# A two-layer decoder trunk on one core: layer 0 with three pairs by token halves, twelve early products and three-pass downs; layer 1 with pairs 0 and 1 by seven, low results by VectorE

## The chip, the core and the metric

The kernel runs on one core of one Trainium2 chip. A core has TensorE (PE) for matmuls, with its weight loads (PEld) shown apart; VectorE (DVE), ScalarE (ACT) and GpSimd (POOL) for elementwise work; and SyncE (SP), which here only issues DMAs. Each engine works through its own queue in order; semaphores make it wait for others. The metric is the device time of one execution in microseconds (us), lower is better.

## What is computed

512 tokens (S) of 1024 channels (D) in float32 go through two layers. Cut to what matters:

```python
h = h + conformer_conv(rmsnorm(h, g0), ...)     # layer 0: pw1, GLU, 31-tap causal conv, LayerNorm, silu, pw2
h = h + swiglu_ffn(rmsnorm(h, g1), w_up[0], w_down[0])
k, v = split(rmsnorm(h, g_kv) @ w_kv)
q = rmsnorm(h, g2) @ w_q                        # layer 1: windowed attention with sinks and a bias
h = h + banded_sink_attention(q, k, v, sinks, rel_bias) @ w_o
h = h + swiglu_ffn(rmsnorm(h, g3), w_up[1], w_down[1])
return rmsnorm(h, g_final)

def swiglu_ffn(x, w_up, w_down):
    gate, up = split(x @ w_up, 2)
    return (silu(gate) * up) @ w_down           # hidden width 2816
```

The change touches the two feed-forward networks (FFN) and what runs beside them.

## The kernel before

**Pairs and chunks.** The 2816 hidden columns are worked on as 11 pairs of 256 columns. Weights come as chunks of 128 x 1024 floats (512 KB) in a list written out beforehand, `PLAN` (`chunk_plan`): 258 chunks. `load` (L261) issues each as a DMA on SP's queue into one of six `raw` buffers, up to nine chunks ahead of use. ScalarE then rounds a chunk to its high half `whi` (L294), and VectorE subtracts to get the low half `wlo` (L297), three chunks ahead of use. A product is made of three passes of TensorE, high by high, high by low and low by high (`mm3`, L380, L381, L382). `get` and `get_seven` hand out the next chunk and call `advance`, which issues loads, splits and a share of the weight sums.

**By seven.** A pair's up matmul can be done directly, four chunks of 24 matmuls on 512 tokens, or "by seven": the weight blocks A11, A12, A21, A22 and the activation blocks B are combined as in Strassen's method into seven products, each of one chunk (24 matmuls of 256 tokens). The combinations are named in

```python
SEVEN = ("A11 B11", "S1 T1", "S2 T2", "A12 B21", "S3 T3", "S4 B22", "A22 T4")
```

S1 to S4 are sums of weight blocks. They are made in DRAM ahead of time by `prepare`: a copy on SP's queue (L275) and a DMA on POOL's queue that adds the other block (L289). `share[0]` says how many such sums are started per chunk used. Some copies are made early in larger pieces (`EARLY`). T1 to T4 are sums of activation blocks. The products of a pair are added up in PSUM chains and in an `up` tile (`SevenPair.take`), then gated (`gates`).

**Layer 0.** After pw1 and the convolution, the tokens are done in two halves of 256. `HALVES0` names which pairs go by halves (`HALVES0[0]`) and which by seven on all 512 tokens (`HALVES0[1]`). The first half runs pw2, its direct pairs and their downs with 256-wide matmuls, then a few "early" by-seven products that need the first half alone (`FIRST`); then pw2 of the second half; then the second half's direct pairs as "twins" (`mm2`, L412, L413): one 512-wide matmul takes the high half of the weights with the activations' high and low halves side by side, one 256-wide takes the low half of the weights. Twin downs do the same. Then come all remaining by-seven products, `part2_products`, and their downs with 512-wide matmuls. The rest of the convolution's second half and other background work is spread over the products by `job` and its points (`pace`).

**Layer 1.** After keys, values, queries, attention and output, `STEPS1` gives the order of the FFN: ups of a pair, and "low" steps, in which two pairs' downs are done by seven as well (L902), each pass in three matmuls of 512 columns. Pair 0 goes directly (`plain_pair`), the other ten by seven. GpSimd makes layer 1's T sums (L759). The results of a low product are scaled and added to `h` by VectorE, those of A12 by ScalarE (L908) and GpSimd (L909).

The order within a queue is that of the code, with a few orderings between engines forced by `tc.issue_after`.

## Time and profile before

| what | value |
|---|---|
| time, median of 3 (lowest to highest) | 1044.0 us (1043.8 to 1045.36) |
| time of the profiled execution | 1043.27 us |
| its span, first to last instruction | 1041.5 us |
| mean granted TensorE clock | 0.997 |
| TensorE busy | 1031.5 us (99%) |
| VectorE / ScalarE / GpSimd busy | 776.5 / 613.0 / 473.2 us |
| moved by DMA | 248.33 MB |

The profile is one execution. In its windows each engine's busy time stands with the instructions that ran in the window; a group of instructions is named by its line of the kernel, engine, operation and tiles, `out<-in`. The stages that matter below, in us from the span's start: the first half's ups 172 to 207 and downs to 230, the early products to about 240, pw2 of the second half to 267, twins 267 to 335, by-seven products 335 to 468, their downs 468 to 544, key to output 544 to 698, layer 1's pair 0 from 698 to 720.

### The profile page before, as it was taken

What the parts mean: (1) busy time and instruction counts of PE and PEld (TensorE: products, weight loads), DVE (VectorE), ACT (ScalarE), POOL (GpSimd) and SP (SyncE); (2) the same over time, 40 slices, a digit from 0 to 9 for tenths busy, and PEclk for the clock granted to TensorE, in tenths of its full rate; (3) what the DMA queues carried; (4) which work ended last, traced back from release to release, by engine and by line L of the source; (5) the groups of instructions that cost most, each with busy time, mean ns of one, the idle gap of its engine ahead of it and who ended that gap; (6) DMA issues with size and microseconds to landing.
All of it is one profiled execution on the core that took longest, in us unless ns stands there. A gap on an engine that the chain in (4) does not pass through costs nothing.

```text
span 1041.5 us, 17709 instructions
## 1 busy us (share of the span) xinstructions
PE 1031.5 (99%) x6580; PEld 932.6 (90%) x6580; DVE 776.5 (75%) x1202; ACT 613.0 (59%) x1062; POOL 473.2 (45%) x569
## 2 busy tenths in 40 slices
...
DMA  9999747999999988999969766955879988877742
GB/s 356 340 315 207 205 126 204 272 256 275 249 239 262 304 220 284 256 301 244 286 209 254 210 183 183 228 154 152 252 230 312 287 264 264 245 233 222 224 150 81
DMA packets 67282, 248.33 MB, mean 238 GB/s; under 512 B 7579, under 2 KB 13884, under 8 KB 66364
## 3 DMA queue, kind: packets, MB, share of 16 engines
...
q10 hardware_dynamic: 288, 0.31, 0.1%
...
## 4 chain that ended last, share of the span: by engine, by line
PE 98%; DMA 0%; DVE 0%; issue 0%; POOLq 0%; SPq 0%; POOL 0%; ACT 0%
PE bank L380 20%; PE bank L382 20%; PE bank L381 20%; PE bank L960 10%; PE bank L902 9%; PE bank L412 4%; PE bank L378 4%; PE bank L413 2%; PE bank L1441 1%; PE bank L1483 1%; PE bank L1470 1%; PE bank L1058 1%; PE bank L1607 1%; PE bank L948 1%; DMA both<-in_lead_dram 0%; PE bank L1562 0%
## 5 line engine op out<-in xcount | busy, mean ns | idle before, releaser
L297 DVE TENSOR_TENSOR wlo<-raw,whi 128x1024 fp32r<-128x1024 f32 x246 | 329.7, 1348 | 136.8 <-ACT whi L294 136.5
L294 ACT CAST whi<-raw 128x1024 fp32r<-128x1024 f32 x246 | 257.1, 1049 | 276.6 <-PE bank L381 194.1
L380 PE MATMUL bank<-quad,whi 128*128 128x256 f32 (+1 forms) x976 | 307.4, 317 | 0.0
L381 PE MATMUL bank<-quad,whi 128*128 128x256 f32 (+1 forms) x976 | 306.6, 315 | 0.0
L382 PE MATMUL bank<-quad,wlo 128*128 128x256 f32 (+1 forms) x976 | 305.7, 315 | 0.0
L380 PEld LDWEIGHTS bank<-quad,whi 128*128 128x128 f32 x976 | 185.5, 191 | 12.8 <-issue 1.6
L381 PEld LDWEIGHTS bank<-quad,whi 128*128 128x128 f32 x976 | 186.0, 191 | 11.9 <-issue 0.5
L382 PEld LDWEIGHTS bank<-quad,wlo 128*128 128x128 f32 x976 | 185.6, 191 | 11.8 <-issue 0.4
L853 POOL TENSOR_TENSOR up<-up 128x512 f32<-128x512 f32 x34 | 62.9, 1851 | 283.6 <-ACT up L850 283.6
L1002 POOL TENSOR_TENSOR pr<-pr,pr 128x256 f32<-128x256 f32 x208 | 155.4, 788 | 2.6 <-ACT pr L1001 2.5
L380 PE MATMUL bank<-rows,whi 128*128 128x256 f32 x488 | 138.0, 283 | 0.0
L381 PE MATMUL bank<-rows,whi 128*128 128x256 f32 x488 | 137.8, 282 | 0.0
L382 PE MATMUL bank<-rows,wlo 128*128 128x256 f32 x488 | 137.8, 282 | 0.0
L1009 DVE SCALAR_TENSOR_TENSOR bank<-apad,wdw,bank 128x256 f32<-128x256 f32 x248 | 112.4, 485 | 3.4
L1001 ACT ACTIVATE pr<-apad,wdw 128x256 f32<-128x256 f32 x208 | 98.3, 502 | 14.9 <-POOL pr L1002 13.1
L960 PE MATMUL bank<-quad,w 128*128 128x256 f32 x448 | 98.7, 380 | 0.0
L960 PEld LDWEIGHTS bank<-quad,w 128*128 128x128 f32 x448 | 84.9, 190 | 11.8 <-DVE bank L1009 0.2
L380 PEld LDWEIGHTS bank<-rows,whi 128*128 128x128 f32 x488 | 93.1, 191 | 0.3
L381 PEld LDWEIGHTS bank<-rows,whi 128*128 128x128 f32 x488 | 93.1, 191 | 0.3
L382 PEld LDWEIGHTS bank<-rows,wlo 128*128 128x128 f32 x488 | 93.0, 191 | 0.0
L491 POOL TENSOR_TENSOR tmp<-tmp,tmp 128x256 f32<-128x256 f32 (+1 forms) x28 | 26.8, 957 | 101.4 <-ACT tmp L487 96.2
L412 PE MATMUL bank<-quad,whi 128*128 128x512 f32 x168 | 59.7, 398 | 0.0
(230 smaller groups left out, 1635.9 us busy)
## 6 DMA issues: line engine op xcount, KB each, us to landing
raw<-in_W_dram SPq DMA_DIRECT2D x170, 512.0 KB, 5.7
raw<-sum SPq DMA_DIRECT2D x88, 512.0 KB, 5.4
sum<-in_W_dram SPq DMA_DIRECT2D x52, 512.0 KB, 6.2
sum<-in_W_dram POOLq DMA_DIRECT2D x44, 512.0 KB, 9.6
sum<-sum POOLq DMA_DIRECT2D x44, 512.0 KB, 8.5
...
w<-in_W_dram SPq DMA_DIRECT2D x14, 512.0 KB, 8.6
...
```

The source lines that it names most:

```text
L294: on_act = nc.scalar.copy(hi, src).ins
L297: latest[:] = [on_act, lo_engine[0].tensor_sub(lo, src, f32(hi)).ins]
L380: nc.tensor.matmul(out, w[0], x[0], start=start, stop=False, **kw)
L381: nc.tensor.matmul(out, w[0], x[1], start=False, stop=False, **kw)
L382: nc.tensor.matmul(out, w[1], x[0], start=False, stop=stop, **kw)
L412: nc.tensor.matmul(first[2], first[0], first[1], start=start, stop=False)
L853: pool_op(nc.gpsimd.tensor_mul(gate, gate, c[:, m, :, 1, :]))
L902: nc.tensor.matmul(out, x, w[:, ws], start=first and e == 0 and i == 0, stop=e == 1 and i == 2, skip_group_check=True)
L960: mm = nc.tensor.matmul(self.pb[:, w * W2:(w + 1) * W2], w1_of(ct, w, k), x[k] if x else xg[k][:, tok], start=k == 0, stop=k == KT - 1)
L1001: on_act = nc.scalar.mul(pr, a[:, j:j + W2], tap(j))
L1002: on_pool = pool_op(nc.gpsimd.tensor_add(pr, acc, pr))
L1009: on_dve = nc.vector.scalar_tensor_tensor(yt if i == nd - 1 else c, src, tap(i), c if i else self.shift, op0=ALU.mult, op1=ALU.add)
```

## The change

It does these things:

- Layer 0's pair 3 moves from the pairs by halves to those by seven (3 and 8 pairs in place of 4 and 7). The eight pairs are worked in two groups of four, each followed by its own downs.
- There are twelve early products in place of three: A12 of all eight pairs and A11 of four. ScalarE copies their results out; four of the tiles for them come from a new pool, `keep`. A11 and A12 of a pair share a bank. `part2_products` then has 21 products in the first group and 23 in the second, where there were 46.
- The second half's downs are no longer twins: they use `mm3` with 256-wide matmuls, and their results are taken out by VectorE two at a time (`held`, `let_go`).
- Layer 1's pair 0 goes by seven. Pairs 0 and 1 are interleaved in the order `TWO`, with S4 in a chain of its own (`apart`), and the T sums move from GpSimd to VectorE (L749).
- The results of low A12 products are scaled and added by VectorE like the others.
- The share of sums per chunk rises: 0.45 to 0.5 in the halves, 0.25 to 0.45 in the by-seven products of layer 0, 1 to 1.2 from keys to output. The number of sums rises from 88 to 96. The job points are set anew.

The number of chunks stays 258, of which 246 are split. Line numbers of the changed kernel are one or so off: L260, L293 and L296 are load, cast and subtraction, L381 to L383 the three passes, L274 and L288 copy and sum.

```diff
-HALVES0 = ((0, 4), (4, 11))
-FIRST = (4, 5, 6)
+HALVES0 = ((0, 3), (3, 11))
+GROUPS0 = ((3, 7), (7, 11))
+FIRST11 = (4, 5, 6, 7)
+FIRST = [(4, "A11"), (3, "A12"), (4, "A12"), (5, "A11"), (8, "A12"), (5, "A12"),
+         (6, "A11"), (9, "A12"), (6, "A12"), (7, "A11"), (10, "A12"), (7, "A12")]
 LAST = FT // 2 - 1
-STEPS1 = [("up", 0), ("up", 1), ("up", 2), ("low", 0)]
+STEPS1 = [("two", 0), ("up", 2), ("low", 0)]
+TWO = [(p, a) for a in ("A11", "A12", "S4") for p in range(2)] + [(p, a) for p in range(2) for a in ("S1", "S2", "S3", "A22")]
 for _p in range(3, LAST, 2):
     STEPS1 += [("up", _p), ("up", _p + 1), ("low", _p - 1)]
...
-def part2_products():
+def part2_products(group):
 
     steps, held = [], []
-    for pair in range(*HALVES0[1]):
+    for pair in range(*group):
         names = [n.split()[0] for n in SEVEN]
-        if pair in FIRST:
-            names = ["A11", "S1", "S2", "S4", "S3", "A22"]
+        names = ["A11", "S1", "S2", "S4", "S3", "A22"][pair in FIRST11:]
         steps += [(pair, names[0])] + held
-        held = [(pair, names.pop())] if pair in FIRST else []
+        held = [(pair, names.pop())]
         steps += [(pair, n) for n in names[1:]]
     return steps + held
...
+    held = []
+
+    def let_go():
+        b, rs_bc, into = held.pop(0)
+        nc.vector.tensor_mul(b, b, rs_bc)
+        nc.vector.tensor_add(into, b, into)
+
     def ffn_part(layer, part, xg, tok, rms, on_h=None, twin=False, plain=None):
         lo, hi = HALVES0[part]
         hid = ffn_up(layer, lo, hi, xg, tok, rms, twin, plain)
         w = tok.stop - tok.start
         for g in range(2):
-            if twin:
-                banks = [bank().rearrange("p (a s) -> p a s", a=2) for _ in range(4)]
-                for kp in range(lo, hi):
-                    whi, wlo = get("down", layer, kp, g)
-                    order = [(k, m) for k in range(2) for m in range(4)]
-                    if kp == hi - 1:
-                        order = [(k, m) for m in range(4) for k in range(2)]
-                    for k, m in order:
-                        sl = slice(m * P, (m + 1) * P)
-                        mm2(banks[m], (whi[:, k, sl], wlo[:, k, sl]), hid.both(2 * (kp - lo) + k),
-                            kp == lo and k == 0, kp == hi - 1 and k == 1)
-                rs_bc = rms.step2()
-                for m, b in enumerate(banks):
-                    t, hm = temp()[:, 0:w], h[g * 4 + m][:, tok]
-                    nc.scalar.copy(t, b[:, 1, :])
-                    nc.vector.tensor_add(t, b[:, 0, :], t)
-                    pool_op(nc.gpsimd.tensor_mul(t, t, rs_bc))
-                    nc.vector.tensor_add(hm, hm, t)
-                continue
             if w == 256:
 
                 full = [bank().rearrange("p (a s) -> p a s", a=2) for _ in range(2)]
@@ -617,11 +606,10 @@
             if w == 256:
                 rs_bc = rms.step2().unsqueeze(1).to_broadcast([P, 2, w])
                 for e, b in enumerate(full):
-                    i = g * 4 + 2 * e
-                    nc.vector.tensor_mul(b, b, rs_bc)
-                    nc.vector.tensor_add(hT[:, i:i + 2, tok], b, hT[:, i:i + 2, tok])
-                    for k in range(2 if on_h is not None else 0):
-                        on_h(i + k)
+                    into = hT[:, g * 4 + 2 * e:g * 4 + 2 * e + 2, tok]
+                    held.append((b, rs_bc, into))
+                    if twin:
+                        let_go()
                 continue
...
-            for name, t, f, a, b in (("T1", t1, nc.gpsimd.tensor_sub, b11, b12), ("T2", b11, nc.gpsimd.tensor_add, b22, t1),
-                                     ("T3", b12, nc.gpsimd.tensor_sub, b22, b12), ("T4", b21, nc.gpsimd.tensor_sub, b11, b21)):
-                pool_op(f(t, a, b))
+            yield
+            for name, t, f, a, b in (("T1", t1, nc.vector.tensor_sub, b11, b12), ("T2", b11, nc.vector.tensor_add, b22, t1),
+                                     ("T3", b12, nc.vector.tensor_sub, b22, b12), ("T4", b21, nc.vector.tensor_sub, b11, b21)):
+                with tc.issue_after(latest[1]):
+                    f(t, a, b)
...
-    def plain_pair(pair, rows, pool):
-
...
+            chain = "w" if self.apart and a == "S4" else CHAINS[a][0]
...
-                if a == "A12":
-                    m = temp()
-                    nc.scalar.mul(m, out, scale)
-                    pool_op(nc.gpsimd.tensor_add(to, to, m.rearrange("p (i c) -> p i c", i=4)))
-                else:
-                    nc.vector.scalar_tensor_tensor(to, src, scale, to, op0=ALU.mult, op1=ALU.add)
+                nc.vector.scalar_tensor_tensor(to, src, scale, to, op0=ALU.mult, op1=ALU.add)
...
+    kept = ExitStack()
+    keep = kept.enter_context(tc.tile_pool(name="keep", bufs=4))
...
-        preparing[0], share[0] = prepare(), 0.45
+        preparing[0], share[0] = prepare(), 0.5
...
-        first = quad(F32)
-        first = {pair: first[:, n, :].rearrange("p (a s) -> p a s", a=2) for n, pair in enumerate(FIRST)}
-        for pair in FIRST:
+        for _ in range(2):
+            let_go()
+        room = [q[:, n, :] for q in (quad(F32), quad(F32)) for n in range(4)]
+        room[4:4] = [keep.tile([P, 512], F32, tag="c11", name=uid("c11")) for _ in range(4)]
+        room = [t.rearrange("p (a s) -> p a s", a=2) for t in room]
+        first = {pair: {"A12": room[n]} for n, pair in enumerate(range(*HALVES0[1]))}
+        for n, pair in enumerate(FIRST11):
+            first[pair]["A11"] = room[8 + n]
+        chains = {}
+        for n, (pair, a) in enumerate(FIRST):
             pace()
-            r = new_chain()
-            product(("up0", pair, "A12"), [[x0["ffn0"][4 + k][e][:, HALF[0]] for k in range(4)] for e in range(2)], r, True)
-            nc.scalar.copy(first[pair], r)
+            if n < 2:
+                let_go()
+            begins = pair not in chains
+            r = chains.setdefault(pair, new_chain() if begins else None)
+            j = 4 * (a == "A12")
+            product(("up0", pair, a), [[x0["ffn0"][j + k][e][:, HALF[0]] for k in range(4)] for e in range(2)], r, begins, pace)
+            nc.scalar.copy(first[pair][a], r)
...
-    share[0] = 1 / 4
...
+    share[0] = 0.45
+    for group in GROUPS0:
+        lo0, hi0 = group
+        last = hi0 == HALVES0[1][1]
+        hid0, open_pairs = [], {}
+        left = [n for n, _ in part2_products(group)]
+        for pair, a in part2_products(group):
+            if pair not in open_pairs:
+                if pair % 2:
+                    c = quads.tile([P, 2, 2, 2, 256], F32, tag="quad", name=uid("up"))
...
+        flush()
+        if last:
+            part2.close()
+            kept.close()
+            attn = ExitStack()
+            at = attn.enter_context(tc.tile_pool(name="attn", bufs=2))
+            job(chain(*(read_bias(*b) for b in ((0, 0), (0, 1), (1, 0)))), (seen[0], 0), (seen[0] + 7, 7))
+            share[0] = 0.6
         for g in range(2):
             banks = accs(512)
             down_group([(("down", 0, kp, g), 2 * (kp - lo0)) for kp in range(lo0, hi0)], lambda kt: hid0[kt], banks)
             for m in range(4):
                 nc.vector.tensor_add(h[g * 4 + m], banks[m], h[g * 4 + m])
-                nxt.on_h(g * 4 + m)
+                if last:
+                    nxt.on_h(g * 4 + m)
...
-        share[0] = 1
+        share[0] = 1.2
...
+        if kind == "two":
+            two = [SevenPair("up", p, nxt, new_gates(pool7), apart=True) for p in range(2)]
+            steps = nxt.sums()
+            for n, (p, a) in enumerate(TWO):
+                two[p].take(a)
+                if n == 3:
+                    nxt.rms.step1()
+                for _ in range((1, 2)[n in (2, 3, 4, 5)]):
+                    next(steps, None)
+                if n >= 6:
+                    flip()
+                if a == "A22":
+                    forms[p] = forms_of(two[p].gates(), pool7, p % 2)
+            continue
+        c = seven_pair("up", pair, nxt, new_gates(pool7))
         if pair != LAST:
```

In three places the order of instructions shows it.

On SP's queue, among the by-seven products of layer 0: `raw` is a chunk (from the weights or from a finished sum), `sum` a copy for a sum to come. Before:

```order
L261 DMA raw_4198<-in_W_dram 128x1024
L261 DMA raw_4229<-sum_507 128x1024
L261 DMA raw_4260<-sum_509 128x1024
L261 DMA raw_4291<-in_W_dram 128x1024
L275 DMA sum_4324<-in_W_dram 16x8192
L261 DMA raw_4327<-in_W_dram 128x1024
L261 DMA raw_4358<-sum_503 128x1024
L261 DMA raw_4404<-sum_505 128x1024
L261 DMA raw_4435<-in_W_dram 128x1024
L275 DMA sum_4467<-in_W_dram 16x8192
```

After, in the first group:

```order
L260 DMA raw_4466<-sum_506 128x1024
L274 DMA sum_4496<-in_W_dram 16x8192
L260 DMA raw_4499<-sum_508 128x1024
L260 DMA raw_4529<-sum_512 128x1024
L274 DMA sum_4559<-in_W_dram 16x8192
L260 DMA raw_4562<-sum_510 128x1024
L260 DMA raw_4600<-in_W_dram 128x1024
L274 DMA sum_4630<-in_W_dram 16x8192
L260 DMA raw_4633<-in_W_dram 128x1024
L260 DMA raw_4663<-sum_506 128x1024
L274 DMA sum_4693<-in_W_dram 16x8192
```

A copy stands behind every two or three chunks in place of every four.

On TensorE, the second half's downs. Before, twin pairs (L412, L413), each pair on one activation tile:

```order
L412 MATMUL bank_3055<-quad_1395,whi_3081 128x512
L412 MATMUL bank_3052<-quad_1395,whi_3059 128x512
L413 MATMUL bank_3052<-quad_1395,wlo_3060 128x256
L412 MATMUL bank_3052<-quad_1396,whi_3059 128x512
L413 MATMUL bank_3052<-quad_1396,wlo_3060 128x256
L412 MATMUL bank_3052<-quad_1396,wlo_3060 128x256
```

After, three passes of 256 columns each:

```order
L381 MATMUL bank_3517<-quad_3158,whi_3456 128x256
L382 MATMUL bank_3517<-quad_3158,whi_3456 128x256
L383 MATMUL bank_3517<-quad_3158,wlo_3457 128x256
L381 MATMUL bank_3517<-quad_3158,whi_3456 128x256
L382 MATMUL bank_3517<-quad_3158,whi_3456 128x256
L383 MATMUL bank_3517<-quad_3158,wlo_3457 128x256
```

One pair of a 512-wide and a 256-wide matmul has become three 256-wide ones.

At the opening of layer 1. Before, GpSimd's queue had the T sums, and a copy's sum between them:

```order
L759 TENSOR_TENSOR t_7441<-quad_7431 128x1024
L289 DMA sum_6958<-sum_6331 128x1024
L759 TENSOR_TENSOR quad_7431<-quad_7432,t_7441 128x4x256
L759 TENSOR_TENSOR quad_7431<-quad_7432,quad_7431 128x4x256
L759 TENSOR_TENSOR quad_7432<-quad_7431,quad_7432 128x4x256
```

and VectorE's had the splits of T (`rows`) among the weight subtractions (`wlo`) and the norm's small work:

```order
L297 TENSOR_TENSOR wlo_7449<-raw_7176,whi_7448 128x1024
L545 TENSOR_TENSOR rows_7476<-t_7441,rows_7476 128x1024
L505 TENSOR_SCALAR ms_7395<-bank_7390 128x4
L542 SCALAR_TENSOR_TENSOR rows_7480<-quad_7431,rows_7480 128x1024
L545 TENSOR_TENSOR rows_7514<-quad_7431,rows_7514 128x1024
L297 TENSOR_TENSOR wlo_7487<-raw_7209,whi_7486 128x1024
L510 TENSOR_TENSOR tmp_7399<-ident,rs_7397 128x512
L1571 TENSOR_SCALAR nrs<-rs_7397 128x4
```

After, VectorE's queue at that place has the T sums (L749) too, and the first results of pairs 0 and 1 (L808):

```order
L749 TENSOR_TENSOR t_7438<-quad_7428 128x1024
L296 TENSOR_TENSOR wlo_7476<-raw_7211,whi_7475 128x1024
L749 TENSOR_TENSOR quad_7428<-quad_7429,t_7438 128x4x256
L808 TENSOR_TENSOR up_7394<-bank_7472,up_7394 128x512
L296 TENSOR_TENSOR wlo_7515<-raw_7244,whi_7514 128x1024
L749 TENSOR_TENSOR quad_7428<-quad_7429,quad_7428 128x4x256
L808 TENSOR_TENSOR up_7395<-bank_7508,up_7395 128x512
L506 TENSOR_SCALAR ms_7548<-bank_7543 128x4
L546 TENSOR_TENSOR rows_7504<-t_7438,rows_7504 128x1024
L296 TENSOR_TENSOR wlo_7562<-raw_7304,whi_7561 128x1024
L749 TENSOR_TENSOR quad_7429<-quad_7428,quad_7429 128x4x256
```

The four sums have moved behind and between the subtractions on VectorE; GpSimd has none of them left.

153 lines of the change are left out of this document (65 added, 88 removed).

## The prediction, before the changed kernel had run

> **What bounds the kernel now.** I read the page first (parts 1, 2 and 4), then the windows of its stages, then groups, transfers and waits.
>
> ```profile
> span 1041.5 us, 17709 instructions
> PE 1031.5 (99%) x6580; PEld 932.6 (90%) x6580; DVE 776.5 (75%) x1202; ACT 613.0 (59%) x1062; POOL 473.2 (45%) x569
> DMA  9999747999999988999969766955879988877742
> PE 98%; DMA 0%; DVE 0%; issue 0%; POOLq 0%; SPq 0%; POOL 0%; ACT 0%
> ```
>
> TensorE is busy for 1031.5 of 1041.5 us, and the chain that ended last lies on it for 98%. So nothing that only makes another engine faster can gain. Time is won by fewer or shorter matmuls, and lost when TensorE has to wait for something. The DMA row stands at 8 or 9 tenths in most slices from the middle of the kernel's first half on: transfers are the second resource to watch.
>
> A matmul's recorded duration overlaps its neighbours', so I price a matmul by its spacing: the length of a window divided by the records in it. These windows lie inside stages:
>
> ```profile
> 172.00:207.00 35.00, 35.00 (x288) 34.79 (x287) 32.73 (x44) 28.10 (x51) 33.16 (x38) 1.00 0.99 270
> 267.00:335.00 68.00, 68.00 (x390) 59.24 (x389) 59.52 (x70) 47.20 (x79) 29.12 (x28) 1.00 0.95 263
> 308.00:330.00 22.00, 22.00 (x127) 19.17 (x126) 21.80 (x27) 14.60 (x23) 7.63 (x7) 1.00 0.88 247
> 335.00:468.00 133.00, 133.00 (x1101) 132.25 (x1100) 98.59 (x113) 74.29 (x98) 39.28 (x29) 1.00 0.92 270
> 350.00:410.00 60.00, 60.00 (x505) 60.00 (x504) 43.18 (x50) 34.22 (x45) 16.63 (x11) 1.00 0.90 272
> 468.00:544.00 76.00, 76.00 (x348) 63.42 (x347) 31.03 (x32) 24.77 (x32) 14.66 (x18) 1.00 0.85 257
> 480.00:530.00 50.00, 50.00 (x222) 41.42 (x221) 19.33 (x19) 14.17 (x17) 9.42 (x13) 1.00 0.93 262
> 698.00:720.00 22.00, 22.00 (x103) 18.14 (x101) 18.56 (x16) 14.50 (x20) 12.24 (x6) 1.00 0.37 97
> 820.00:900.00 80.00, 80.00 (x525) 73.40 (x524) 61.73 (x69) 42.10 (x53) 30.78 (x26) 1.00 0.86 276
> ```
>
> The columns are the window and its length; busy time and instructions of TensorE, of its weight loads, of VectorE, ScalarE and GpSimd; then the granted clock, the busy share of the DMA engines and GB/s. The clock is 1.00 everywhere. One record at an edge belongs to the neighbouring window, so I divide by one less:
>
> - a 256-wide matmul: 60.00 / 504 = 119.0 ns (in the window from 172, where it is the ups of the first half, 35.00 / 287 = 121.9);
> - a 512-wide matmul of three passes: 50.00 / 221 = 226.2 ns;
> - a twin pair (one 512-wide, one 256-wide): 2 x 22.00 / 126 = 349.2 ns.
>
> The forms and their counts before:
>
> ```profile
> L380 PE MATMUL bank<-quad,whi 128*128 128x256 f32 x688 | 195.2, 286 | 0.0
> L380 PE MATMUL bank<-rows,whi 128*128 128x256 f32 x488 | 138.0, 283 | 0.0
> L380 PE MATMUL bank<-quad,whi 128*128 128x512 f32 x288 | 112.1, 393 | 0.0
> L412 PE MATMUL bank<-quad,whi 128*128 128x512 f32 x168 | 59.7, 398 | 0.0
> L413 PE MATMUL bank<-quad,whi 128*128 128x512 f32 x24 | 9.5, 396 | 0.0
> ```
>
> L380 is one pass of three, so these are 3 x (688 + 488) 256-wide matmuls, 3 x 288 512-wide ones, and 168 + 24 = 192 twin pairs; idle before each is 0.0.
>
> **The sum, term by term (TensorE).** A weight chunk is 24 matmuls in three passes, or 8 twin pairs.
>
> 1. Ups of layer 0's pair 3. Before: four chunks for the first half (96 256-wide) and four as twins (32 pairs). After: seven products of 24. 72 x 119.0 - 32 x 349.2 ns = 8.57 - 11.17 = -2.6 us.
> 2. Downs of that pair. Before two chunks 256-wide (48) and two as twins (16 pairs); after two chunks 512-wide (48). -5.71 - 5.59 + 10.86 = -0.4 us.
> 3. Twin downs of pairs 0 to 2 become three passes: 48 pairs out, 144 256-wide in. 17.14 - 16.76 = +0.4 us.
> 4. Layer 1's pair 0: 96 512-wide out, 168 256-wide in. 19.99 - 21.72 = -1.7 us.
>
> Together +336 256-wide, -48 512-wide and -96 pairs: 39.98 - 10.86 - 33.52 = **-4.4 us**. With 121.9 for each new 256-wide matmul it is 40.96 - 44.38 = -3.4; I take 119.0, since that window is nearest in place to most of the new products, and keep -3.4 as an end. The twelve early products, of which three existed, are products drawn forward: no matmul more.
>
> The profiled execution took 1043.27 us, 0.73 under the median of 1044.0. So -4.4 gives 1038.9 against its own time and **1039.6** against the median.
>
> **What moves beside TensorE.** Each of these I cost at nothing for the cover named.
>
> ```profile
> L297 DVE TENSOR_TENSOR wlo<-raw,whi 128x1024 fp32r<-128x1024 f32 x246 | 329.7, 1348 | 136.8 <-ACT whi L294 136.5
> L834 ACT COPY up<-bank 128x512 f32<-128x512 f32 x17 | 9.9, 580 | 0.0
> L1547 DVE TENSOR_TENSOR h<-bank,h 128x512 f32<-128x512 f32 x8 | 5.5, 686 | 0.8 <-PE bank L382 0.8
> L908 ACT ACTIVATE tmp<-bank,rs 128x512 f32<-128x512 f32 x10 | 6.8, 684 | 3.1 <-PE bank L902 3.0
> L911 DVE SCALAR_TENSOR_TENSOR h<-bank,rs,h 128x512 f32<-128x512 f32 x30 | 22.0, 746 | 9.1 <-PE bank L902 9.1
> ```
>
> - Nine more early results copied by ScalarE: 9 x 0.58 = 5.2 us, at about 2.9 us (24 x 119 ns) of TensorE per product, so under a quarter of its time. If it were late, the next chain of that bank would wait 0.6 us.
> - Eight more residual adds after the first group's downs: 8 x 0.69 = 5.5 us of VectorE, in a stage like 468 to 544, where it is busy for 31.03 of 76.
> - Twin downs: ScalarE's copy and GpSimd's product go, and VectorE works on pairs of results, with fewer instructions, so the tight window from 308 (21.80 of 22) only gets lighter.
> - Ten low results go from ScalarE and GpSimd to VectorE: 10 x 0.75 = 7.5 us over layer 1's ups; in the window from 820, 61.73 of 80 is busy, and two more per low step make it about 63 to 65.
> - GpSimd's four T sums become VectorE's, below.
> - DMAs: 8 more copies and 8 more accumulations, and a higher share of them per chunk (0.25 to 0.45 in the by-seven products of layer 0), below. SP's queue is passed by 12 more small copies, POOL's by 8 more issues.
>
> **Rival 1, on the other side: transfers come late in layer 0's products.** Queue 1 carries weights and copies, queue 0 accumulations. First the stretch with share 0.45 and no copies, 267 to 335, then that with 0.25 and copies, 335 to 468:
>
> ```profile
> q0 software_dynamic: 1582, 5.76, 48.0%
> q1 hardware_dynamic: 3312, 12.06, 46.8%
> ```
>
> ```profile
> q1 hardware_dynamic: 7014, 28.74, 60.9%
> q0 software_dynamic: 1934, 7.01, 30.8%
> ```
>
> A transfer is 0.524 MB. In the first, 11 accumulations cost 0.48 x 68 / 11 = 2.97 us of the sixteen engines each, 23 others 1.38; in the second, 3.06 and 1.48. A product lasts 2.86 us. At share 0.45 with copies the engines need 1.38 + 0.45 x (2.97 + 1.38) = 3.34 us, or by the second 3.52: short by 0.48 to 0.66 us in each, 10 to 14 us over the 21 products of the first group, 11 to 15 over the 23 of the second. These costs hold waiting inside a transfer, so they are upper ends; the lower end is no shortage, since the window from 172 ran at 0.99 with TensorE busy throughout. The 8 chunks of downs behind each group (5.4 us each) repay it. Against the shortage stands the lead:
>
> ```profile
> raw<-in_W_dram SPq DMA_DIRECT2D x170, 512.0 KB, 5.7
> ```
>
> ```profile
> ACT whi L294 <- PE bank L381: 194.1, 103, 4.4
> ACT whi L294 <- DMA raw<-in_W_dram: 4.4, 1, 4.4
> ```
>
> ```profile
> 352.78 1.05 ACT L294 CAST whi<-raw 128x1024 fp32r<-128x1024 f32 x1 [0.38 <-DMA raw<-sum]
> ```
>
> Six buffers at 2.86 us are 17 us, less 5.7 to land leaves 11; the cast runs three chunks ahead of its product, which after cast (1.05) and subtraction (1.35) leaves 6 more. ScalarE's casts wait for TensorE to give buffers back (194.1 us), for a weight transfer once. But at 352.78 a cast did start the moment its chunk landed, so bursts already eat the 11 us. Shortage 0 to 15 plus bursts of 11 against 17: a stall of 0 to 9 us per group, in PE's queue at the first matmul of a product, with all later work behind it. From 2.3 us in both together the change is no longer visibly faster; above 6.5 it is slower. Taking 5 us in one group and 4 in the other, 1039.6 + 9 = 1048.6.
>
> **Rival 2: VectorE is late at the opening of layer 1.**
>
> ```profile
> L297 DVE TENSOR_TENSOR wlo<-raw,whi x4: 1212/1213/8075, 706.0 to 721.5; 128x1024 fp32r<-128x1024 f32 x4
> ```
>
> ```profile
> 702.66 2.41 POOL L759 TENSOR_TENSOR t<-quad 128x1024 f32<-128x1024 f32 x1 [34.98 <-ACT quad L753]
> 705.57 2.67 POOL L759 TENSOR_TENSOR quad<-quad,t 128x1024 f32<-128x1024 f32 x1
> 707.93 5.01 POOL L759 TENSOR_TENSOR quad<-quad,quad 128x1024 f32<-128x1024 f32 x2
> ```
>
> One subtraction took 8.07 us, not 1.21, while GpSimd ran the T sums. After, VectorE has in some 38 us: 13 subtractions, 4 T sums and 4 T splits (21 x 1.21 = 25.4), and 13 operations of 0.69 (9.0): 34.4, or 91%. TensorE waits for each T and each subtraction in turn, so one late by a microsecond costs that. From below nothing, from above the four T sums in full, 4.8 us: 1039.6 to 1044.4. I take nothing: the stretched 8.07 leaves with the GpSimd sums. The same small wait can come from rival 1's lower part; with 2 to 4.8 us, both land at 1041.6 to 1044.4.
>
> **Rival 3: the count of matmuls, not their columns, sets the time.** There are 336 - 48 - 192 = 96 matmuls more, each with its weight load. Loads fill 60.00 of 60.00 us in the 256-wide window, 41.42 of 50 in the 512-wide one. The gain is gone once a new 256-wide matmul takes 44.38 / 336 = 132.1 ns, against 119.0 to 121.9 in the rows. With 135, +1.0 us: 1045.0.
>
> The Trainium skill ("TensorE: Matmul & The Clock Gate", section "Back-to-back issue gap") speaks for this: it gives a sustained spacing of about 81 ns for 128 columns and 131 for 512, so that width counts little. A straight line between these (an estimate from that page) would give 98 ns at 256 columns and a sum of +4.6 us. Our rows, 119.0 and 226.2, differ from it and go by columns, so the rival keeps a small chance.
>
> **How the numbers follow.** No new stall above 1 us: 0.62 (1038.3 to 1041). Small waits, rivals 1 and 2: 0.18, of which 0.03 still below 1041.9. Rival 1 in full: 0.15. Rival 3: 0.05, half of it slower. A measurement of this kernel tells about 0.2%, 2.1 us, from no change: 1041.9 and 1046.1 are the bounds. Faster 0.62 + 0.03 = 0.65; same 0.15 + 0.02 = 0.17; slower 0.15 + 0.03 = 0.18. The range runs from 1038.2, a little below the sum, to 1046.2, and leaves out the slower cases alone; the likeliest one's own is 1038.3 to 1041.
>
> **What would show it.** TensorE's busy time should fall by 4 to 5 us and its idle time stay near 10. A right sum shows counts x spacing as in the four terms. Rival 1 would show ScalarE's casts waiting for raw transfers, and TensorE idle behind L296 or the casts, between the two groups' starts and ends. Rival 2 would show TensorE waiting for VectorE in layer 1's first 40 us. Rival 3 would show a 256-wide spacing above 122 ns. I am wrong if TensorE idles elsewhere: at the new early products, whose results must be out before their bank goes on.

## The result and the profile after

The changed kernel takes 1042.91 us (median of 21 runs, 1042.18 to 1043.99), the kernel before beside it 1044.37 us (21 runs, 1043.8 to 1045.46). The ratio is 0.9985, with a 95% interval of 0.9979 to 0.9990: faster by 1.5 us, less than the 0.2%, or 2.1 us, that I had called visible. The forecast was 1039.6 us. The profiled execution took 1043.35 us.

The page of the profile after, as the prediction showed it for before:

```profile
span 1041.6 us, 17905 instructions
PE 1029.7 (99%) x6676; PEld 935.2 (90%) x6676; DVE 794.5 (76%) x1228; ACT 603.4 (58%) x1044; POOL 455.3 (44%) x557
DMA  9999847999999999889998987977699897655642
PE 94%; DVE 3%; DMA 2%; issue 1%; ACT 0%; POOLq 0%; POOL 0%; ACTq 0%; DVEq 0%
```

TensorE's busy time fell by 1.8 us, not by 4 to 5, and it is idle for 11.9 us, not 10. The chain that ended last now runs over VectorE and a DMA for 5% of the span, where it lay on TensorE for 98%. So there are new waits. First, did the sum hold? Windows of the changed kernel inside one kind of matmul (columns as in the prediction):

```profile
277.00:294.00 17.00, 17.00 (x99) 14.83 (x98) 11.90 (x16) 13.23 (x29) 6.22 (x8) 1.00 1.04 278
350.00:388.00 38.00, 38.00 (x322) 38.00 (x321) 35.76 (x44) 22.13 (x29) 11.34 (x9) 1.00 0.99 312
434.00:495.00 61.00, 61.00 (x510) 60.84 (x509) 46.51 (x53) 32.79 (x41) 18.85 (x14) 1.00 0.89 283
510.00:550.00 40.00, 40.00 (x179) 33.10 (x178) 25.02 (x27) 20.18 (x30) 14.28 (x16) 1.00 0.96 289
```

38.00 / 321 = 118.4 and 61.00 / 509 = 119.8 ns for a 256-wide matmul in the by-seven products, 40.00 / 178 = 224.7 ns for a 512-wide one, 2 x 17.00 / 98 = 346.9 ns for a twin pair: the prices of the sum within 1%. Where the time went shows at four marks on TensorE's timeline: the first up of layer 0, the first matmul of keys and values, the first one after attention's values, and the last. Before:

```profile
172.17 0.47 PE L380 MATMUL bank<-quad,whi 128*128 128x256 f32 x1
...
554.87 0.37 PE L380 MATMUL bank<-whi,quad 128*128 128x256 f32 x1
...
675.99 0.50 PE L382 MATMUL bank<-quad,wlo 128*128 128x512 f32 x1
...
1033.05 0.28 PE L1607 MATMUL bank<-whi,hid 128*128 128x256 f32 x1
```

and after:

```profile
170.95 0.47 PE L381 MATMUL bank<-quad,whi 128*128 128x256 f32 x1
...
556.00 0.37 PE L381 MATMUL bank<-whi,quad 128*128 128x256 f32 x1
...
677.11 0.50 PE L383 MATMUL bank<-quad,wlo 128*128 128x512 f32 x1
...
1033.20 0.28 PE L1612 MATMUL bank<-whi,hid 128*128 128x256 f32 x1
```

Layer 0 takes 382.70 us before and 385.05 after, +2.35, where the sum said -2.6. The stretch up to the values' end is the same (121.1). From there to the last matmul it is 357.06 and 356.09: -0.97, where the sum said -1.7. The new waits, on the same timeline (the bracket holds the idle time before the matmul and what ended it):

```profile
203.43 0.38 PE L382 MATMUL bank<-quad,whi 128*128 128x256 f32 x1 [0.37 <-DVE quad L546]
...
231.23 0.39 PE L381 MATMUL bank<-quad,whi 128*128 128x256 f32 x1 [0.17 <-ACT quad L1245]
...
318.46 0.39 PE L383 MATMUL bank<-quad,wlo 128*128 128x256 f32 x1 [0.93 <-DVE wlo L296]
...
339.43 0.39 PE L381 MATMUL bank<-rows,whi 128*128 128x256 f32 x1 [0.42 <-ACT whi L293]
...
735.10 0.39 PE L381 MATMUL bank<-rows,whi 128*128 128x256 f32 x1 [0.18 <-DVE up L810]
```

A bracket counts from the modelled end of the matmul before; measured as start-to-start time over the usual spacing, and with the neighbours that were late too, these places cost 0.74, 0.43, 1.56, 1.17 and 0.45 us. I call them the waits at 202, 231, 317, 336 and 735; 0.42 more lie in two small ones near 175 and 181. Below, a wait is always counted this way.

Layer 0 then adds up. Four of its matmuls for statistics, two that read `yy` and two that read its squares, stood ahead of the first up before and stand behind it after. All that read `yy`, with the first and the last start, before:

```profile
L1052 PE MATMUL bank<-yy,ones_m x4: 377/378/379, 161.1 to 205.1; 128*128 128x256 f32 x4
```

and after:

```profile
L1025 PE MATMUL bank<-yy,ones_m x4: 378/378/462, 174.4 to 220.2; 128*128 128x256 f32 x4
```

By their spacings the four that moved are 0.7 us. All gaps above the usual spacing are 1.5 us in layer 0 before and 5.8 after. So -2.6 + 0.7 + 4.3 = +2.4, as measured; and layer 1 has -1.7 + 0.8 = -0.9 against -0.97. Of these 0.8 us, 0.45 are the wait at 735 and 0.10 one at 790; the rest is small, and most of it is that a 256-wide matmul takes 0.120 us there, not 0.119. The stage ahead of the first up gets the same 0.7 us shorter; that it is 1.22 shorter here says little, since its length spreads by 1.2 us among the executions of kernels that share its code. The matmul sum was right to about 0.3 us. The question is what makes the waits.

### The profile page after: what moved, and what is told of

Same layout as the page of the kernel before. It is cut to its first block, busy times and chain, and to the rows that moved or that the text cites. A ratio compares the mean times of both kernels' runs of the same rounds, so it can differ in the third digit from the quotient of the medians.

```text
span 1041.6 us, 17905 instructions
## 1 busy us (share of the span) xinstructions
PE 1029.7 (99%) x6676; PEld 935.2 (90%) x6676; DVE 794.5 (76%) x1228; ACT 603.4 (58%) x1044; POOL 455.3 (44%) x557
## 4 chain that ended last, share of the span: by engine, by line
PE 94%; DVE 3%; DMA 2%; issue 1%; ACT 0%; POOLq 0%; POOL 0%; ACTq 0%; DVEq 0%
PE bank L381 20%; PE bank L382 20%; PE bank L383 20%; PE bank L933 10%; PE bank L878 9%; PE bank L379 4%; PE bank L413 2%; DMA raw<-sum 1%; PE bank L1437 1%; PE bank L1479 1%; PE bank L1466 1%; DVE wlo L296 1%; PE bank L414 1%; PE bank L1031 1%; PE bank L1612 1%
## 5 line engine op out<-in xcount | busy, mean ns | idle before, releaser
L293 ACT CAST whi<-raw 128x1024 fp32r<-128x1024 f32 x246 | 256.5, 1048 | 275.1 <-PE bank L382 181.0
L296 DVE TENSOR_TENSOR wlo<-raw,whi 128x1024 fp32r<-128x1024 f32 x246 | 317.6, 1299 | 117.3 <-ACT whi L293 116.5
L381 PE MATMUL bank<-quad,whi 128*128 128x256 f32 (+1 forms) x1016 | 315.8, 314 | 0.3 <-ACT quad L1245 0.2
L382 PE MATMUL bank<-quad,whi 128*128 128x256 f32 (+1 forms) x1016 | 315.5, 312 | 0.4 <-DVE quad L546 0.4
L383 PE MATMUL bank<-quad,wlo 128*128 128x256 f32 (+1 forms) x1016 | 314.5, 312 | 0.9 <-DVE wlo L296 0.9
L829 POOL TENSOR_TENSOR up<-up 128x512 f32<-128x512 f32 x38 | 71.8, 1889 | 345.9 <-ACT up L826 319.3
L381 PEld LDWEIGHTS bank<-quad,whi 128*128 128x128 f32 x1016 | 192.9, 191 | 13.1 <-issue 1.3
L383 PEld LDWEIGHTS bank<-quad,wlo 128*128 128x128 f32 x1016 | 193.0, 191 | 12.4 <-DVE wlo L296 1.1
L382 PEld LDWEIGHTS bank<-quad,whi 128*128 128x128 f32 x1016 | 193.4, 191 | 11.6 <-DVE quad L546 0.6
L381 PE MATMUL bank<-rows,whi 128*128 128x256 f32 x544 | 154.0, 284 | 0.7 <-ACT whi L293 0.4
L382 PE MATMUL bank<-rows,whi 128*128 128x256 f32 x544 | 153.6, 283 | 0.0
L383 PE MATMUL bank<-rows,wlo 128*128 128x256 f32 x544 | 153.4, 283 | 0.0
L381 PEld LDWEIGHTS bank<-rows,whi 128*128 128x128 f32 x544 | 103.5, 191 | 1.9 <-ACT whi L293 0.6
L382 PEld LDWEIGHTS bank<-rows,whi 128*128 128x128 f32 x544 | 103.7, 191 | 0.5 <-issue 0.2
L383 PEld LDWEIGHTS bank<-rows,wlo 128*128 128x128 f32 x544 | 103.6, 191 | 0.0
L878 PE MATMUL bank<-wlo,fhi 128*128 128x512 f32 x140 | 55.3, 395 | 0.0
## 6 DMA issues: line engine op xcount, KB each, us to landing
sum<-sum POOLq DMA_DIRECT2D x48, 512.0 KB, 10.3
```

Of the source, the lines that this page charges most:

```text
L293: on_act = nc.scalar.copy(hi, src).ins
L296: latest[:] = [on_act, lo_engine[0].tensor_sub(lo, src, f32(hi)).ins]
L381: nc.tensor.matmul(out, w[0], x[0], start=start, stop=False, **kw)
L382: nc.tensor.matmul(out, w[0], x[1], start=False, stop=False, **kw)
L383: stamp[0] = nc.tensor.matmul(out, w[1], x[0], start=False, stop=stop, **kw).ins
L829: pool_op(nc.gpsimd.tensor_mul(gate, gate, c[:, m, :, 1, :]))
```

## Experiments

**Each half of the change alone, and before once more.** l1_only puts the layer-1 part and the new share from keys to output into the kernel before; l0_only undoes that part in the changed kernel; before_again is the kernel before without an edit.

```diff
 # l1_only, against before
-STEPS1 = [("up", 0), ("up", 1), ("up", 2), ("low", 0)]
+STEPS1 = [("two", 0), ("up", 2), ("low", 0)]
...
 # l0_only, against after
-STEPS1 = [("two", 0), ("up", 2), ("low", 0)]
+STEPS1 = [("up", 0), ("up", 1), ("up", 2), ("low", 0)]
```

> The kernel before with the layer-1 part of the change alone (pairs 0 and 1 by seven and interleaved, T sums and low A12 results by VectorE; the share of sums from keys to output is 1.2, as in the changed kernel, because the sums are needed earlier). Theory A (the matmul sum was right, waits of TensorE in layer 0 gave most of it back): -1.7 us of matmuls and one wait of about 0.35 us near the opening of layer 1, so 1.2 to 1.7 us under before, 1042.7 to 1043.2. Theory B (a new 256-wide matmul costs more than 119 ns, every term shrinks to a third): about 0.6 us under before, 1043.8.

> The changed kernel with its layer-1 part undone (pair 0 direct, T sums on GpSimd, low A12 results by ScalarE and GpSimd). Theory A: -2.7 us of matmuls, and the waits at 202, 231, 317 to 320 and 336 to 340 us are all still there, about 3 us, so before -0.7 to before +0.7, 1043.7 to 1045.1. Theory B: -0.9 us and no waits that matter, 1043.5.

> The kernel before once more, for a second profile. Its first profiled execution took 1043.27 us, under the median of all its later runs (1044.4 to 1044.9). Theory F (the first one was a fast execution, and most others lose about a microsecond in a wait of the first half): TensorE waits 1 to 1.4 us near 199 us, as in the profile of the kernel with the layer-1 part alone, and the time is 1044.2 to 1045. If the first profile was typical: no such wait, and the difference lies around the span.

l1_only: 1043.68 us, ratio 0.9990 (0.9982 to 0.9999), with the wait at 735 and none of the changed kernel's waits in layer 0. l0_only: 1044.07, 0.9995 (0.9986 to 1.0003), with those at 202, 231, 317, and 0.22 at 336. Layer 1 from the values' end is about 0.97 us shorter in every kernel with the layer-1 part. before_again, 1044.77 in its one execution, showed a wait that the first profile of before lacked:

```profile
200.75 0.39 PE L382 MATMUL bank<-quad,wlo 128*128 128x256 f32 x1 [1.00 <-DVE wlo L297]
```

It costs 1.26 us, stands in l1_only too, and by itself makes before_again's TensorE work 1.25 us longer than in the profile that I predicted from. That profile was of one of before's shorter executions. No trace of a kernel with the changed layer 0 has it; most have the 0.74 at 202 near the place. So part of the 1.5 us is probably this wait, but how many of before's timed executions have it is not shown. The medians of before that were taken beside the runs lie between 1043.81 and 1045.18 us from one group of runs to another. So kernels of different groups that differ by less than about 1 us are told apart here by their traces, not by their times.

**VectorE or transfers? Accumulations taken away or made small.** no_adds drops the accumulating DMAs; thin_adds cuts each to 128 of 1024 columns, so that the issue stays and seven eighths of the bytes go.

```diff
 # no_adds
-            with tc.issue_after(pooled[0]):
-                nc.gpsimd.dma_start(summed[c], chunk(c, SUMS[c[2]][1]), accum_op=ALU.add, max_dma_last_dim=4096)
...
 # thin_adds
-                nc.gpsimd.dma_start(summed[c], chunk(c, SUMS[c[2]][1]), accum_op=ALU.add, max_dma_last_dim=4096)
+                nc.gpsimd.dma_start(summed[c][:, 0:128], chunk(c, SUMS[c[2]][1])[:, 0:128], accum_op=ALU.add, max_dma_last_dim=4096)
```

> The changed kernel without the accumulating DMAs (GpSimd's queue), so the weight sums are not summed and the output is not the reference's; copies, loads and all matmuls stay. Theory A and C: the wait for a raw transfer at 336 to 340 goes, and VectorE's operations there are not stretched by GpSimd's issues, 1.0 to 2.0 us less than the changed kernel, 1041 to 1042; the wait at 202, which is VectorE's, stays. Theory B: within 0.3 us of the changed kernel.

> The changed kernel in which every accumulating DMA moves 128 of its 1024 columns: as many issues on GpSimd's queue, an eighth of their bytes (the weight sums are summed in these columns alone, so the output is not the reference's). It tells apart what the accumulations cost: the bytes on the DMA engines (theory C) or GpSimd's issues, beside which VectorE's operations run longer (theory D). Without the accumulations the time was 3.7 us under before, against about 1.5 for the changed kernel. Theory C: 3.0 to 3.7 us under before, 1041.2 to 1041.9, and the waits at 202 and 336 to 340 gone. Theory D: 1.2 to 2.0 us under before, the wait at 202 still there.

no_adds: 1041.19 us, 0.9963 (0.9949 to 0.9977); the waits at 202 and 231 are gone, 317 has 0.83 and 336 0.23. thin_adds: 1043.43, 0.9992 (0.9983 to 1.0001); 202 (0.74), 231 (0.41) and 317 (1.55) stay, 336 has 0.21. So in these traces 336 hangs on the bytes of the accumulations, 202 and 231 on their being issued at all, and so does half of 317. Layer 0 of thin_adds is 0.92 us shorter in its trace than that of after (384.13 and 385.05), but as a whole it was no faster.

What stands behind 231 can be read further. ScalarE in after, where `[...<-POOL y]` is a wait for GpSimd's part of the convolution and L1245 the copy of an early result:

```profile
229.34 0.42 ACT L1011 ACTIVATE sq<-y 128x256 f32<-128x256 f32 x1 [1.26 <-POOL y L986]
...
230.60 0.58 ACT L1245 COPY quad<-bank 128x512 f32<-128x512 f32 x1
```

GpSimd's two operations L986, in after:

```profile
226.89 2.42 POOL L986 TENSOR_TENSOR y<-y,pr 128x256 f32<-128x256 f32 x2 [7.38 <-DVE y L982]
```

and in no_adds, where that line is L984:

```profile
224.48 1.43 POOL L984 TENSOR_TENSOR y<-y,pr 128x256 f32<-128x256 f32 x2 [5.61 <-DVE y L980]
```

The convolution's second half comes later and slower through GpSimd with accumulations in its queue; ScalarE waits for it, and the early result queued behind is copied late, so that the next product waits for its bank.

**When and where the T sums of layer 0 are made.** They run on VectorE in the second half. t_late draws T2 to T4 back by one to four chunks, t34_late T3 and T4 alone, t_early draws them forward; t1_quad gives T1 a tile of its own instead of a raw buffer.

```diff
-    job(rows0.sums(), (base + 10, 0), (base + 14, 8), (base + 17, 10), (base + 20, 12), (base + 23, 14), (base + 26, 15), (base + 29, 17))
 # t_late
+    job(rows0.sums(), (base + 10, 0), (base + 14, 8), (base + 17, 10), (base + 21, 10), (base + 24, 12), (base + 27, 14), (base + 28, 15), (base + 31, 17))
 # t34_late
+    job(rows0.sums(), (base + 10, 0), (base + 14, 8), (base + 17, 10), (base + 20, 12), (base + 25, 12), (base + 27, 14), (base + 29, 15), (base + 31, 17))
 # t_early
+    job(rows0.sums(), (base + 10, 0), (base + 12, 8), (base + 14, 10), (base + 16, 12), (base + 19, 14), (base + 23, 15), (base + 27, 17))
...
 # t1_quad
-            t1 = wpool.tile([P, 4, 256], F32, tag="raw", name=uid("t1"), bufs=6)
+            t1 = quad(F32)[:, :, 0:256]
```

> The changed kernel with the T sums of layer 0 (VectorE, L1283) issued later: T2 to T4 among the second half's downs and the first products, not among its twin ups. Theory A, with VectorE as the cause of the wait at 317 to 320: that wait goes, 1.0 to 1.4 us less than the changed kernel, 1041.5 to 1041.9; the wait at 336 to 340 stays or shrinks. If only transfers count (theory C): within 0.3 us of the changed kernel, 1042.9. The new danger is that a T is late for its product, which would show as TensorE waiting for rows.

> The changed kernel with T1 and T2 of layer 0 where they were, so that T1's raw buffer comes back as before, and T3 and T4 (sums and splits, 4 operations of 1.2 us and two of 0.7 on VectorE) moved to the last downs and the first products. Theory A (VectorE's full stretch from 298 to 337 us makes the wait at 317 to 320): that wait falls under 0.5 us, 0.8 to 1.3 us less than the changed kernel, 2.2 to 2.9 under before. Theory D (GpSimd's operations and issues there make it, whatever VectorE has to do): it stays at 1.0 or more, 1.2 to 1.8 under before.

> The changed kernel with the T sums of layer 0 earlier, from the first of the second half's ups on, where VectorE is busy for 11.9 of 17 us. Theory A (VectorE is full from 298 to 337 us): the wait of 1.5 us at 317 to 320 goes or falls under 0.4, T1 gives its raw buffer back sooner, 1.0 to 2.0 us less than the changed kernel, 2.4 to 3.5 under before. If GpSimd's issues cause that wait wherever the T sums stand (theory D): it falls to about 0.8, 0.5 to 0.8 us gained.

> The changed kernel with layer 0's T1 in a tile of its own, not in one of the six raw buffers that the loads use. Theory E (T1 holds a raw buffer from its sum to T2's, so a load is issued some 7 us late and the lead over TensorE is gone): casts at 338 to 350 no longer start as their chunk lands, the wait at 336 to 340 goes, 0.8 to 1.2 us less than the changed kernel, 2.3 to 2.7 under before. If the transfers are late by their number alone (theory C): within 0.3 us of the changed kernel, 1.2 to 1.8 under before.

t_late: 1051.61, 1.0066 (1.0053 to 1.0078). t34_late: 1050.06, 1.0044 (1.0030 to 1.0058). t_early: 1044.95, 1.0002 (0.9993 to 1.0011). t1_quad: 1043.85, 0.9996 (0.9987 to 1.0005). The two late ones do shrink 317, to about 0.5, so VectorE's T work is what is late there. But 336 grows to 6.8 and 6.3 us. The waits of t34_late by what ended them (total, times, longest):

```profile
PE bank L381 <- ACT whi L293: 6.1, 1, 6.1
```

t_early moves the wait at 317 to 310 and 316 (0.85 and 2.51); t1_quad leaves 317 and has 0.83 at 336. None gains. In t34_late TensorE waits at 336 for a cast that itself waited 4.04 us for its chunk, so what grows there is a late transfer. With fewer accumulations as well (best2, below) that wait is 1.56 us, and the one at 317 is gone.

**What VectorE does there.** In the changed kernel it is full. Windows of after:

```profile
294.00:311.00 17.00, 17.00 (x99) 14.85 (x98) 16.12 (x15) 11.74 (x19) 9.30 (x8) 1.00 0.89 213
311.00:320.00 9.00, 8.07 (x66) 7.76 (x64) 9.00 (x10) 5.06 (x8) 4.79 (x3) 1.00 1.03 290
320.00:333.00 13.00, 12.90 (x108) 12.75 (x107) 13.00 (x17) 7.00 (x10) 4.53 (x6) 1.00 1.04 274
```

Part of this is no work. VectorE's timeline of after:

```profile
306.25 2.31 DVE L1283 TENSOR_TENSOR plain<-plain,t 128x1024 f32<-128x1024 f32 x1
...
313.16 1.21 DVE L296 TENSOR_TENSOR wlo<-raw,whi 128x1024 fp32r<-128x1024 f32 x1
314.29 2.32 DVE L1283 TENSOR_TENSOR plain<-plain 128x1024 f32<-128x1024 f32 x1
...
318.32 2.31 DVE L546 TENSOR_TENSOR rows<-plain,rows 128x1024 fp32r<-128x1024 f32 x1
```

and GpSimd's in the same stretch:

```profile
305.34 2.14 POOL L637 TENSOR_TENSOR tmp<-tmp,tmp 128x512 f32<-128x512 f32 x1 [3.64 <-DVE tmp L633]
...
313.32 2.21 POOL L635 TENSOR_TENSOR tmp<-tmp,rsbc 128x512 f32<-128x512 f32 x1 [4.22 <-DVE tmp L633]
317.42 2.13 POOL L637 TENSOR_TENSOR tmp<-tmp,tmp 128x512 f32<-128x512 f32 x1 [1.89 <-DVE tmp L633]
319.50 0.82 POOL L288 DMA_DIRECT2D sum<-in_W_dram  x1
320.05 1.95 POOL L288 DMA_DIRECT2D sum<-sum  x2
321.09 2.57 POOL L288 DMA_DIRECT2D sum<-in_W_dram  x2
322.15 2.38 POOL L288 DMA_DIRECT2D sum<-sum  x1
```

A VectorE operation of the usual 1.21 us that starts while L635 or L637, the twins' gating, is running lasts until that one's end and 1.08 us more: 305.34 + 2.14 + 1.08 = 308.56, and L1283 ends at 308.56; 313.32 + 2.21 + 1.08 = 316.61 and 316.61; 317.42 + 2.13 + 1.08 = 320.63 and 320.63. The 8.07 us subtraction of the kernel before fits as well: it starts at 705.96, and GpSimd's sums end at 712.94. Over this stretch VectorE loses some 5.6 us so. The Trainium skill ("GPSIMD Engine Reference", section "1. Specifications") says that GpSimd shares its SBUF interfaces with VectorE, with contention where a VectorE instruction has two inputs in SBUF (the on-chip memory of the tiles). The rows agree: the three operations have two such inputs and take 2.31 to 2.32 us in place of 1.21.

The same rows show 336. Accumulations wait in GpSimd's queue behind L637, which waits for VectorE's L633, and then go out together from 319.50 on. The chain of after, from there:

```profile
323.53 14.69 DMA raw<-sum
338.32 1.06 ACT whi L293
339.43 0.39 PE bank L381
```

A chunk issued at 323.53 lands after 14.69 us, where the median for such chunks (`raw<-sum`) was 5.4 before; its cast, then TensorE, wait for it. The size of this wait is one execution's: l0_only issues the same DMAs there, its chunk, issued at 323.83, was cast at 337.42, some 1.2 us sooner after its issue, and TensorE lost 0.22 us. The place stands on an edge, and which size is the usual one is not shown.

**The two causes told apart: gating on VectorE, fewer accumulations.** gate_dve gives L635 and L637 to VectorE; share_late sets the share of sums in the second half's ups and downs from 0.5 to 0.2; gate_dve_share does both.

```diff
 # gate_dve
-                nc.gpsimd.tensor_mul(t1v, t1v, rs_bc.unsqueeze(1).to_broadcast([P, 2, w]))
+                nc.vector.tensor_mul(t1v, t1v, rs_bc.unsqueeze(1).to_broadcast([P, 2, w]))
                 nc.scalar.activation(t1, t1, AF.Silu)
-                pool_op(nc.gpsimd.tensor_mul(t2, t1, t2))
+                nc.vector.tensor_mul(t2, t1, t2)
...
 # share_late, ahead of the second half's ups
+    share[0] = 0.2
```

> The changed kernel with a share of sums of 0.2 in place of 0.5 in the second half's ups and downs (0.45 again in the products). Theory C (transfers crowd there): the late raw transfers at 325 to 340 and TensorE's wait of about 1 us behind them go, 0.7 to 1.2 us less than the changed kernel, 2.2 to 2.7 under before; the 1.5 us at 317 to 320 shrink by what GpSimd's issues stretched. If the delayed sums only move the crowding into the first group: no gain, 1.3 to 1.7 under before, and a wait there.

> The changed kernel with the two multiplications of the twin gating (GpSimd's L635 and L637, 1.9 to 2.2 us each) made by VectorE; three pairs, so six operations of about 0.69 us, 4.1 us more on VectorE, and about 12.6 us less on GpSimd. Theory (VectorE's operations in the second half are stretched to the ends of these two, about 5.6 us in all, and accumulations queue behind L637 and come in a bunch): the operations of 2.31 us fall to about 1.21, the wait near 317 us falls from 1.56 to under 0.6, that near 336 from 1.2 to about 0.2, TensorE's length from its first up falls by about 2 us, and the time to about 1041 us, ratio to before 0.996 to 0.998. Rival (VectorE is full there by its own work, the stretching is idle time anyway): the 4.1 us come on top, the wait near 317 grows to 2.5 to 4 us, and the time is 1044 to 1046 us.

> As gate_dve, and the share of accumulations per chunk in the second half's ups and downs at 0.2. Theory (two separate causes, VectorE's stretched operations at 317 us and the bunched accumulations at 336 us): beside gate_dve at most 0.5 us is to be gained, since GpSimd's queue is free of waiting multiplications already; 1040.5 to 1042 us. Rival (the accumulations matter by their number, not by their place in GpSimd's queue): this one is 1 us or more faster than gate_dve.

> The kernel of gate_dve once more, since its profiled execution was a disturbed one (4260 us, every matmul near 900 ns) and its timed ones had a granted clock of 0.994 to 0.997 where the kernel before beside them had 0.997 to 0.998. With the gating on VectorE and share 0.2 the operations beside it had fallen to 1.22 us and the waits near 317 and 336 us were gone; a wait of 0.56 near 324 stood instead. Theory of the stretched operations and the queued accumulations: alone, with the share of the changed kernel, the same waits are gone too, 1041 to 1042.5 us. Rival (the time is really 1046 to 1047, as the first runs had it, since accumulations now issued freely at the higher share fill the DMA engines while 12 chunks are needed): raw chunks take 15 us or more to land between 295 and 335 us, and TensorE waits 3 to 5 us there behind a cast.

share_late: 1042.57, 0.9986 (0.9977 to 0.9995); 317 has 0.82 and 336 0.22. gate_dve: 1046.96, 1.0030 (1.0021 to 1.0040), and the same kernel as gate_dve_again: 1048.39, 1.0035 (1.0023 to 1.0047), 1045.22 in the profiled execution, the one that is read here. gate_dve_share: 1042.05, 0.9984 (0.9975 to 0.9993). With the gating on VectorE no operation of this stretch is lengthened. The rows of gate_dve_share that answer to the two last long ones:

```profile
312.60 1.22 DVE L1283 TENSOR_TENSOR plain<-plain 128x1024 f32<-128x1024 f32 x1
...
317.88 1.22 DVE L546 TENSOR_TENSOR rows<-plain,rows 128x1024 fp32r<-128x1024 f32 x1
```

The waits at 317 and 336 are gone in both; a wait at 324 stands there, of 0.56 in gate_dve_share and 4.44 in gate_dve_again. So the stretched operations do make 317. Why share_late halves it shows in VectorE's subtraction beside the L635 near 300, in after and in share_late:

```profile
299.75 3.05 DVE L296 TENSOR_TENSOR wlo<-raw,whi 128x1024 fp32r<-128x1024 f32 x1
...
300.47 2.31 DVE L296 TENSOR_TENSOR wlo<-raw,whi 128x1024 fp32r<-128x1024 f32 x1
```

In after two accumulations stand ahead of that L635 in GpSimd's queue, in share_late one (in no_adds none, and 2.32 us). The 0.74 us between them is what the wait at 317 loses, 1.56 to 0.82. But at 336 the rival named for gate_dve_share is right: the number of accumulations counts, not their place in GpSimd's queue. Windows of gate_dve_again:

```profile
294.00:311.00 17.00, 17.00 (x99) 14.81 (x98) 16.62 (x22) 12.81 (x20) 3.18 (x4) 1.00 1.06 270
311.00:320.00 9.00, 9.00 (x76) 8.95 (x76) 9.00 (x12) 5.42 (x7) 0.09 (x1) 1.00 1.05 274
320.00:333.00 13.00, 10.45 (x73) 10.09 (x73) 6.96 (x8) 4.71 (x6) 0.00 (x0) 0.87 1.08 306
```

In the last, VectorE has time to spare (6.96 of 13), and the DMA engines are full throughout (1.05 to 1.08). Freed of GpSimd's multiplications, the accumulations go out earlier, seven of them from 286.86 to 292.8. From 294 to 336 their queue moved 5.22 MB in gate_dve_again, 3.94 in after and 2.52 in gate_dve_share, and the chunks from finished sums took 16.5, 10.3 and 4.5 us to land (medians): at a share of 0.5 there are too many for the chunks that must land in between. ScalarE's cast comes late because its chunk does:

```profile
325.36 1.04 ACT L293 CAST whi<-raw 128x1024 fp32r<-128x1024 f32 x1 [2.25 <-DMA raw<-sum]
```

As I read it, the queue behind L637 only shifts when their number is felt. With the share down as well (gate_dve_share) the stretch is nearly clean, and what is gained over after is too little to tell: 1042.05 beside 1043.81 for before on its chip, a ratio inside after's own interval.

**The share moved forward, and combinations.** share_front starts fewer sums in the first half's ups and downs (0.2), more during the early products (0.85), and 0.5 afterwards. best1 is t_early with shares 0.2, 0.85 and then 0.2; best2 is t34_late with share_late; best3 is best2 with 0.35 in the first half and 0.6 in the early products.

```diff
 # share_front
-        preparing[0], share[0] = prepare(), 0.5
+        preparing[0], share[0] = prepare(), 0.2
...
+        share[0] = 0.85
...
+    share[0] = 0.5
```

> The changed kernel with a share of sums of 0.2 in place of 0.5 in the first half's ups and downs and 0.85 in the early products and the second half's pw2 (0.5 again after it), so GpSimd issues few accumulations beside the convolution's second half. Theory D (GpSimd's issues delay the convolution's steps and stretch VectorE's): the waits at 202 (0.74 us) and 231 (0.43 us) go, 0.6 to 1.2 us less than the changed kernel, 2.1 to 2.7 under before. Theory C (bytes): in the run with thin accumulations these waits stayed, so nothing is gained, and the later crowding costs 0 to 0.5.

> The changed kernel with the earlier T sums of layer 0 and a share of sums of 0.2 in the first half's ups and downs, 0.85 in the early products and pw2, 0.2 in the second half's ups and downs. Theory A with C and D: the waits at 202, 231, 317 and 336 go, and what stays of the loss is 0.8 us in layer 1 and the many small ones; the matmul sum of -4.4 comes through to about 3 to 3.7, 1041.0 to 1041.7. If the delayed sums crowd the first group: a wait of 1 to 3 us between 340 and 400, 1042 to 1044.

> The same, with a share of sums of 0.2 in the second half's ups and downs too. With that share alone the waits at 317 and 336 were 0.8 and 0.2 us. Theory A: both go, only 202, 231 and layer 1's small ones stay, PE's length is 1018.8 to 1019.2 us, 1041.5 to 1042.2. If a T is late for its product: a wait of over 1 us between 337 and 350.

> The same again, with a share of 0.35 in place of 0.5 in the first half's ups and downs and 0.6 in the early products and pw2. Theory D: the waits at 202 and 231 shrink to a half, another 0.3 to 0.7 us less. With 0.2 and 0.85 there, new waits of 1.7, 1.1 and 3.1 us stood at 284, 308 and 318; if crowding sets in at 0.6 already, they come back in part and it is 1 to 3 us slower than without this step.

share_front: 1046.47, 1.0017 (1.0008 to 1.0026): the waits at 202 and 231 are gone, but there are 1.70 near 284, 1.07 near 308 and 3.09 near 318. best1: 1044.98, 0.9998 (0.9989 to 1.0007). best2: 1044.00, 0.9988 (0.9979 to 0.9997). best3: 1046.19, 1.0011 (1.0002 to 1.0020). best1 has t_early's waits and one of 2.46 near 289, best2 1.56 at 336, best3 that and 3.98 near 216. A sum not started in one stage is started in another, and both are full. None beats the changed kernel.

**Twin downs again.** twin_downs brings the second half's downs back as before (the code that the change removes).

```diff
+            if twin:
+                banks = [bank().rearrange("p (a s) -> p a s", a=2) for _ in range(4)]
...
+                    pool_op(nc.gpsimd.tensor_mul(t, t, rs_bc))
+                    nc.vector.tensor_add(hm, hm, t)
+                continue
```

> The changed kernel with the second half's downs as twins again (three pairs). By the third term of the sum -0.4 us of TensorE. Theory A: VectorE, full from 298 to 337, gets 16 operations of 256 columns in place of 8 of 512, about 1 us more, and ScalarE and GpSimd work beside it, so the waits at 317 to 340 grow by 0.5 to 2 us: 1.5 to 0 under before. Theory B (only matmuls count): 1.9 under before.

1046.47, 1.0019 (1.0010 to 1.0028). Term 3 says 0.4 us less on TensorE; by the two ratios the kernel is 0.34% slower than after, some 3.5 us, with a wait of 4.29 in place of 1.17 at 336, behind VectorE's L810 (part of it is a halved clock, told below). Three passes are dearer by themselves and pay here by what they spare VectorE and GpSimd.

## Why the prediction was wrong

Its direction was right and its range held the time, but the gain was a third of the forecast. The direction is in part luck: beside the execution that the prediction started from (1043.27 us) the profiled one of the changed kernel (1043.35) gains nothing, and the measured gain is hardly more than the wait of 1.26 us that this execution lacked.

- **The sum, -4.4 us: right to about 0.3.** Counts and spacings held, and both layers add up with their waits.
- **"So the tight window from 308 only gets lighter": the step that failed.** I looked at what leaves that window and not at what the change pushes into it. The second half has 18 chunks in place of 24, and the T sums and T splits of layer 0, which stood in it before, now stand in a shorter stretch beside the same gating on GpSimd. The result is the wait at 317, 1.56 us where I had put nothing, shown by t_late, t34_late and the two gate_dve kernels; share_late and no_adds show that half of it comes from accumulations ahead of the gating.
- **Rival 1: its mechanism came, at another place and size.** I looked for it in the two product groups, at 0 to 9 us each. There TensorE does not wait. The shortage is at their threshold, where the second half's share of 0.5 meets the products' quicker chunks: 1.17 us in the trace of after, 0.22 in l0_only with the same issues.
- **"POOL's by 8 more issues", costed at nothing: 1.2 us.** The waits at 202 and 231 go with the accumulations' issues (no_adds, share_front) and not with their bytes (thin_adds). I weighed transfers alone. The one at 231 is an early product that waits for the copy of an earlier result, the sign that the prediction named last and priced at 0.6 us; it took 0.43. How the issues make the one at 202 was not isolated, and no run has the changed layer 0 with the old share of 0.45, so that the eight more are what brings them is not shown.
- **Rival 2: its low end.** 0.45 us in layer 1's opening behind VectorE, where I took nothing. With the 0.10 at 790 and the longer spacings, term 4 brought 0.97 in place of 1.7.
- **Rival 3: fell.** 118.4 to 119.8 ns stand against the 132.1 from which it decides. The Trainium skill's spacings of the section "Back-to-back issue gap" ("TensorE: Matmul & The Clock Gate"), which gave it an estimate of +4.6, do not fit these matmuls.
- **Costed at nothing, and nothing:** the eight residual adds and the ten low results, and the early copies but for the one at 231. No new wait above 0.1 us stands behind the first group's downs or in layer 1 after 735.
- **The base.** I shifted the profile by 0.73 to the median as if by chance. Of the 1.50 us between the two profiled executions of before (1043.27 and 1044.77), 1.26 are a wait that the first lacked. One profile of before could not show this.

Together: -4.4, with 3.9 of four new waits, 0.4 of two small ones and 0.8 in layer 1, is +0.7. If most executions of before have the 1.26 that after has not, which is likely but not shown, it is -0.6, against -1.5 measured (-2.2 to -1.0 by the interval). The profiled execution of after, in which the waits were read, lies 0.4 us above its median. With l0_only's 0.22 at 336 in place of 1.17 the sum would be -1.5, an estimate; what the timed executions have there stays open.
